# A matmul loop that opens with VectorE's pair of tiles: head, casts and transfers rearranged

## The chip, the cores and the metric

One core of a Trainium2 chip. The metric is the device time of one execution in microseconds (us). The kernel before took 210.7 us (median of 4 runs, 210.26 to 210.95).

## The reference

```python
batch, m, k, n = 16, 512, 1024, 768
def reference(x, weight, sub_value):      # x [16,512,1024], weight [1024,768], sub_value [16,512,768], float32
    return (np.matmul(x, weight) - sub_value).astype(np.float32)
```

The 16 x 512 rows are one flat list of 8,192 rows, so the work is a product of 8,192 x 1,024 by 1,024 x 768, less a matrix of the size of the result.

## The kernel before

The rows form 64 m tiles. With SEGMENTS (L14) and `view` (L128) a segment of j tiles gives each of the 128 partitions j neighbouring rows, so that one transfer of n tiles moves n x 4,096 bytes (x) or n x 3,072 bytes (sub_value, result) in one run per partition. x lands in a ring of 16 tiles (`x_ring`), sub_value in a ring of 32 tiles (`so_ring`); the result of a tile overwrites its sub_value in place and is sent from there. The weight is staged in the last eight slots of `so_ring`.

What happens to one tile `mi`:

1. **Cast.** ScalarE casts x from float32 to float16 (`cast`, L300, L317).
2. **Transpose.** TensorE needs x with k on the partitions. Two ways exist. For most tiles TensorE transposes four blocks of 128 x 128 float32 words (each word two float16 values) against an identity (`transposes`, L322, L335), and ScalarE copies the result from PSUM to SBUF (L348, the "evac"). For the tiles in ON_DVE and their successors, VectorE transposes a pair of two tiles with 16 block transposes (`transposes_dve`, L353, L368), and ScalarE has no evac. There is one buffer for a transposed pair (`xtp_b`, NXTP = 1).
3. **Matmuls.** 16 matmuls of 128 x 384 columns (`matmuls`, L377, L198): four chunks c of k, two halves r of a chunk, two halves of n. They add up in one of three PSUM buffers (`po_b`).
4. **Finish.** VectorE subtracts: PSUM minus `so_ring` into `so_ring` (`finish`, L412, L417).

Each engine has a queue written out by hand (`Queue`, L40); engines meet through semaphores. A wait sits on the instruction that needs it, and all that stands behind it on the same engine waits too. SyncE (SP) issues all transfers in the order of TRANSFERS (L29). `issue` (L241) adds a transfer to SP's queue as soon as the program text has passed what frees its slot, and it carries its waits: an x transfer waits for the casts of the 16 tiles before, a sub_value transfer for the landing of the results that it overwrites (or for the weight's casts, L285), a result for its last finish.

TensorE's work has a head and a loop. The head (L438 to L473) computes tiles 0 to 3 by hand, interleaved so that each weight chunk is used by several tiles as it lands, with 26 idle matmuls on zeros that keep TensorE busy meanwhile. Tiles 4 and 5 are TensorE-transposed but stand in the pair buffer (EARLY = 4), so that the loop body has one shape; a memset on GpSimd (L476) and two tiny casts at the end (L499) fill up counters for that. The loop (LOOP = (4, 6, 10), L517) is ten turns of six tiles, 4 to 63: a pair from `xtp_b` and four tiles of TensorE's own. VectorE transposes the nine pairs 10, 16, ..., 58. Transposes of tile `mi + 2` stand between the matmuls of tile `mi` (L490); a pair's VectorE transposes are spread behind the finishes of tiles 5, 4 and 3 places before it, six, six and four (L502 to L506).

The loop counts its semaphore targets in registers, with one jump back per turn (`emit_loop`, L69, L101).

## Time and profile before

| | us |
|---|---|
| median of 4 runs (lowest, highest) | 210.7 (210.26, 210.95) |
| the profiled execution's own time | 210.76 |
| its span, first to last instruction | 208.9 |
| TensorE matmul busy / VectorE / ScalarE | 195.4 / 128.1 / 108.8 |
| DMA queue of the transfers, share of 16 engines' span | 97.8% (87.03 MB) |
| last matmul ends | 201.4 |
| last transfer issued, landed | 202.4, 5.2 us later |

The profiled execution stands 0.06 us above the median. Busy matmuls overlap in the profile: a matmul of 384 columns is shown with 326 ns, but in a dense stretch one starts every 0.1625 us. The 1.8 us between span and time lie outside the first and last instruction.

### The profile page before, as it was taken

The page shows a single profiled execution, that of the slowest core. Times are in us where ns is not written, and L with a number is a line of the kernel's source. Part 1 is how long each engine was busy: PE and PEld are TensorE (multiplying, and loading weights), DVE is VectorE, ACT ScalarE, POOL GpSimd, SP SyncE. Part 2 cuts the span into 40 slices and gives each one's busy share as a digit, 9 for nine tenths or more (in the row PEclk, how much of TensorE's full clock was granted, in tenths as well). Part 3 has the DMA queues.
Part 4 walks back from the last instruction along what each step waited for, and adds up shares of the span by engine and source line. Part 5 has one row for each costly group of instructions (what it writes and reads, how often), then busy time and mean ns, then how long its engine had stood idle before and what let it go on. Part 6 is the DMA issues. An engine that isn't in the chain of part 4 may idle for free.

```text
span 208.9 us, 2614 instructions
## 1 busy us (share of the span) xinstructions
PE 195.4 (94%) x1234; PEld 75.5 (36%) x700; DVE 128.1 (61%) x224; ACT 108.8 (52%) x113; POOL 1.0 (0%) x7
## 2 busy tenths in 40 slices
PE   6999799969999999999999999999999999999950
PEld 0233243324434434433442443343344344334310
DVE  2323314975993895597499389369749929943330
ACT  4555758507574761853845667173574646516300
POOL 1000000000000000000000000000000000000000
PEclk9999999999999999999999999999999999999997
DMA  6999999999999999999999999999999999999992
GB/s 234 410 427 434 443 417 436 455 427 434 423 464 408 346 445 448 450 414 406 474 425 417 438 409 442 447 450 416 433 445 392 445 438 433 414 447 438 408 419 119
DMA packets 5620, 87.08 MB, mean 417 GB/s; under 512 B 624, under 2 KB 624, under 8 KB 2032
## 3 DMA queue, kind: packets, MB, share of 16 engines
q1 hardware_dynamic: 5616, 87.03, 97.8%
q8 instruction: 1, 0.02, 0.0%
q14 instruction: 3, 0.02, 0.0%
HBM read 61.87 MB, written 25.17 MB: 417 GB/s over the span
## 4 chain that ended last, share of the span: by engine, by line
PE 75%; DMA 13%; DVE 6%; SPq 3%; issue 1%; DVEq 0%
PE po_b L198 67%; DMA so_ring<-in_sub_value_dram 13%; PE pt_b L335 8%; DVE xtp_b L368 3%; DVE so_ring L417 2%; SPq L298 2%; SPq L262 1%; SPq L553 0%; DVEq L59 0%; SPq L138 0%
## 5 line engine op out<-in xcount | busy, mean ns | idle before, releaser
L198 PE MATMUL po_b<-w_sb,xt_b 128*128 128x384 f16 x704 | 126.0, 326 | 0.9 <-DVE w_sb L265 0.5
L417 DVE TENSOR_TENSOR so_ring<-po_b,so_ring 128x768 f32<-128x768 f32 x64 | 60.6, 956 | 59.5 <-PE po_b L198 38.7
L348 ACT COPY xt_b<-pt_b 128x1024 f16<-128x1024 f16 x44 | 44.5, 1012 | 64.2 <-PE pt_b L335 63.3
L368 DVE STREAM_TRANSPOSE xtp_b<-x16p_b 32x256 f32<-32x256 f32 x144 | 62.7, 435 | 2.3
L198 PE MATMUL po_b<-w_sb,xtp_b 128*128 128x384 f16 x320 | 61.3, 326 | 1.9 <-DVE xtp_b L368 1.7
L397 PEld LDWEIGHTS <-xt_b 128*128 128x128 f16 x352 | 34.4, 98 | 58.5 <-issue 55.0
L317 ACT CAST x_b<-x_ring 128x1024 f16<-128x1024 f32 x46 | 47.2, 1048 | 4.7 <-DMA x_ring<-in_x_dram 4.7
L335 PE MATMUL pt_b<-ident,x_b 128*128 128x128 f32 x184 | 47.5, 273 | 1.5 <-ACT x_b L317 1.4
L335 PEld LDWEIGHTS pt_b<-ident,x_b 128*128 128x128 f32 x184 | 25.4, 141 | 44.7 <-issue 36.8
L317 ACT CAST x16p_b<-x_ring 128x1024 f16<-128x1024 f32 x18 | 18.8, 1046 | 16.1 <-DMA x_ring<-in_x_dram 16.1
L397 PEld LDWEIGHTS <-xtp_b 128*128 128x128 f16 x160 | 15.7, 98 | 20.4 <-issue 18.3
L265 DVE CAST w_sb<-so_ring 128x768 f16<-128x768 f32 x8 | 4.1, 557 | 11.3 <-DMA so_ring<-in_weight_dram 11.3
L198 PE MATMUL po_b<-idle_x,idle_w 128*128 128x512 f16 x26 | 8.0, 458 | 1.7 <-POOL idle_x L178 1.7
L348 ACT COPY xtp_b<-pt_b 128x1024 f16<-128x1024 f16 x2 | 2.0, 1012 | 2.5 <-PE pt_b L335 2.5
L317 ACT ACT_TABLE_LOAD x1 | 1.3, 1283 | 0.9 <-SPq L138 0.9
L427 PEld LDWEIGHTS <-idle_w 128*128 128x128 f16 x4 | 0.4, 99 | 1.7 <-POOL idle_x L178 1.7
L187 DVE TENSOR_TENSOR ident<-along,across 32x32 f32<-32x32 f32 x4 | 0.7, 183 | 0.1
L179 DVE MEMSET ones<- 128x32 f32 x1 | 0.1, 85 | 1.0 <-SPq L138 1.0
L178 POOL MEMSET idle_x<- 128x512 f16 x1 | 0.5, 529 | 0.0
L499 ACT CAST stub<-ident 128x1 f16<-128x1 f32 x2 | 0.4, 194 | 0.0
L184 DVE STREAM_TRANSPOSE across<-along 128x32 f32<-128x32 f32 x1 | 0.2, 211 | 0.0
L177 POOL MEMSET idle_w<- 128x128 f16 x1 | 0.2, 204 | 0.5 <-SPq L138 0.5
(7 smaller groups left out, 0.9 us busy)
## 6 DMA issues: line engine op xcount, KB each, us to landing
so_ring<-in_sub_value_dram SPq DMA_DIRECT2D x7, 3072.0 KB, 24.2
x_ring<-in_x_dram SPq DMA_DIRECT2D x5, 4096.0 KB, 23.8
out_dram<-so_ring SPq DMA_DIRECT2D x6, 3072.0 KB, 29.0
x_ring<-in_x_dram SPq DMA_DIRECT2D x2, 2048.0 KB, 27.1
so_ring<-in_weight_dram SPq DMA_DIRECT2D x4, 768.0 KB, 8.1
x_ring<-in_x_dram SPq DMA_DIRECT2D x1, 3072.0 KB, 28.9
out_dram<-so_ring SPq DMA_DIRECT2D x1, 2688.0 KB, 26.6
x_ring<-in_x_dram SPq DMA_DIRECT2D x2, 1024.0 KB, 24.8
```

Source lines behind the costliest of these rows:

```text
L178: pool.add(lambda: nc.gpsimd.memset(idle_x, 0.0), then=count("idle"))
L187: dve.add(lambda here=here: nc.vector.tensor_tensor(out=ident[here, here], in0=along[here], in1=across[here], op=mybir.AluOpType.is_equal, ...
L198: return nc.tensor.add_instruction(mybir.InstMatmult(name=nc.get_next_instruction_name(), engine=full.engine, ins=list(full.ins), outs=lis ...
L262: sp.add(lambda st=st, at=at: nc.sync.dma_start(out=st, in_=w_c[at]), then=(sem, 16))
L265: lambda at=at, r=r, st=st: nc.vector.tensor_copy(out=w_sb[:, at, r], in_=st[:, r]),
L298: sp.add(lambda here=here, there=there: nc.sync.dma_start(out=here, in_=there), waits, (sem, 16))
L317: act.add(lambda: nc.scalar.copy(out=to, in_=x_in), waits, count("cast"))
L335: pe.add(lambda: nc.tensor.transpose(words, from_, ident), waits, count("turn") if last else None)
L348: act.add(lambda: nc.scalar.copy(out=to, in_=pt_b[:, b]), waits, count("evac"))
L368: dve.add(lambda: nc.vector.transpose(xt[b * Q : (b + 1) * Q, :, a * Q : (a + 1) * Q], x16[a * Q : (a + 1) * Q, :, b * Q : (b + 1) * Q],), ...
L397: pe.add(lambda weights=weights: nc.tensor.ldweights(weights, tile_position=(0, 0)), [w for w in waits if w[0] in ready])
L417: dve.add(lambda: nc.vector.tensor_tensor(out=o, in0=po[:, :, :NS], in1=o, op=mybir.AluOpType.subtract), [landed["s", mi], (counter["mul"] ...
```

## The change

- **No head.** The pair (0, 1) goes to VectorE, so the loop begins at tile 0. VectorE transposes eleven pairs (0, 6, ..., 60). EARLY, the memset, the stub casts and the interleaved head go. x of tile 1 is cast by VectorE, so that both casts of pair 0 run at once; they have a counter of their own, `both`.
- **The loop** (`emit_turns`) has turns that start at tiles 0, 6, ..., 60 and is left in the middle of the fourth tile of the eleventh turn, after half of tile 63. Its body is two blocks, so each turn has two jumps. Tile 63's last two chunks stand behind it.
- **TensorE's transposes** stand in whole tiles: those of `mi + 2` behind chunk 2 of the pair's two tiles, those of the next two tiles together in the middle of the fourth tile.
- **Casts** have new places in ScalarE's order (CAST_AHEAD). Six of the eight weight casts go to ScalarE. The loop's pair tile waits for each half chunk of the weight by itself.
- **Transfers:** 34 in place of 39. The weight comes in two, behind x of tiles 0 to 3; sub_value 32 to 39 now stands ahead of x 32 to 39, and x 48 to 55 is split.
- **Idle matmuls:** 35 at the start, none later (26 before).

```diff
-SEGMENTS = [(0, 1), (1, 7)] + [(at, 8) for at in range(8, 64, 8)]
+SEGMENTS = [(0, 2), (2, 6)] + [(at, 8) for at in range(8, 64, 8)]
+IDLE = 34
+CAST_AHEAD = (6, 7, 4, 4, 3, 3)
+W_ON_ACT = {(0, 0), (0, 1), (1, 0), (1, 1), (2, 0), (3, 0)}
+PERIOD, CUT = 6, (3, 2)
-ON_DVE = frozenset(range(10, 60, 6))
+ON_DVE = frozenset(range(0, 64, 6))
 TRANSFERS = [
+    ('x', 0, 2), ('x', 2, 2), ('w', 0, 2), ('w', 2, 2), ('x', 4, 4), ('s', 0, 2), ('s', 2, 6),
+    ('x', 8, 4), ('x', 12, 4), ('s', 8, 8), ('x', 16, 8), ('s', 16, 8), ('x', 24, 8),
+    ('o', 0, 2), ('o', 2, 6), ('s', 24, 8), ('s', 32, 8), ('x', 32, 8), ('x', 40, 8),
+    ('o', 8, 8), ('o', 16, 8), ('s', 40, 8), ('x', 48, 2), ('x', 50, 6), ('o', 24, 8),
+    ('s', 48, 8), ('x', 56, 8), ('s', 56, 8), ('o', 32, 8), ('o', 40, 8), ('o', 48, 8),
+    ('o', 56, 5), ('o', 61, 2), ('o', 63, 1),
...
+    def emit_turns(self, turns, cut):
...
+        nc.regs_mov(turn, 1)
+        nc.br("turn_first", engines=engines)
+        with nc.body("turn_first", valid_engines=engines):
+            self.emit(first[:cut], bound, after)
+            nc.br_cmp(turn, len(turns), on_true="turn_done", on_false="turn_second", comp_op="IS_EQ", engines=engines)
+        with nc.body("turn_second", valid_engines=engines):
+            self.emit(first[cut:], lambda n, sem, v: bound(n + cut, sem, v), lambda n, sem: after(n + cut, sem))
+            nc.regs_alu(turn, turn, 1, op=mybir.AluOpType.add)
+            nc.br("turn_first", engines=engines)
+        nc.switch_bb("turn_done")
...
+    def cast_w(c):
+        sem, value, first = w_landed[c]
+        for r in range(2):
+            name = "w_act" if (c, r) in W_ON_ACT else "w"
+            to, from_ = w_sb[:, c, r], so_ring[:, first + r]
+            if name == "w":
+                dve.add(lambda to=to, from_=from_: nc.vector.tensor_copy(out=to, in_=from_), [(sem, value)], count(name))
+            else:
+                act.add(lambda to=to, from_=from_: nc.scalar.copy(out=to, in_=from_), [(sem, value)], count(name))
...
-        act.add(lambda: nc.scalar.copy(out=to, in_=x_in), waits, count("cast"))
+        name = "both" if first in ON_DVE else "cast"
+        if mi == 1:
+            dve.add(lambda to=to, from_=x_in: nc.vector.tensor_copy(out=to, in_=from_), waits, count(name))
+        else:
+            act.add(lambda: nc.scalar.copy(out=to, in_=x_in), waits, count(name))
...
         for r in range(2):
+            if mi % PERIOD == 0:
+                waits.append(w_at[c, r])
...
+    idle(IDLE)
+    cast(0)
+    cast(1)
+    for f in transposes_dve(0):
+        f()
+    cast(2)
+    cast(3)
+    for c in range(n_c):
+        cast_w(c)
+    casts = {0: [6, 7], 1: [4], 2: [5]}
+    for mi in range(8, n_mt):
+        casts.setdefault(mi - CAST_AHEAD[mi % PERIOD], []).append(mi)
...
+    for mi in range(n_mt):
+        for c in range(n_c):
+            if (mi % PERIOD, c) == CUT:
+                marks.append(len(pe.ops))
+                for t in (mi + 1, mi + 2):
+                    if t < n_mt:
+                        transpose_tile(t)
+            matmuls(mi, c)
+            if c == TURN_AT and mi % PERIOD < 2:
+                transpose_tile(mi + TA)
+        for t in casts.get(mi, []):
+            cast(t)
+        finish(mi)
```

The rest of the main loop (VectorE's transposes behind the finishes of 5, 4 and 3 tiles before a pair) is as before.

## The prediction

> **What bounds the kernel now.** I read the page's chain first, then its slices, then the last microseconds of DMA. The chain names TensorE for three quarters of the span:

> ```profile
> PE 75%; DMA 13%; DVE 6%; SPq 3%; issue 1%; DVEq 0%
> ```

> The slices say that the transfers are never short of work either; only the first and last slice fall below full:

> ```profile
> DMA  6999999999999999999999999999999999999992
> GB/s 234 410 427 434 443 417 436 455 427 434 423 464 408 346 445 448 450 414 406 474 425 417 438 409 442 447 450 416 433 445 392 445 438 433 414 447 438 408 419 119
> ```

> The end decides between the two. This is DMA in 40 slices from 202.4 us, when the last transfer (384 KB of tile 63) is issued, to the end of the span:

> ```profile
> DMA  9999998989899984311121201101000000000000
> GB/s 451 395 395 507 413 413 376 451 376 395 338 395 470 376 338 188 132 75 75 56 94 75 94 38 56 56 38 75 38 19 0 0 0 0 0 0 0 0 0 0
> ...
> out_dram<-so_ring SPq DMA_DIRECT2D x1, 384.0 KB, 5.2
> ```

> The engines stay full for 2.5 us after that issue (202.4 to 204.9), so older transfers were ahead. Then a few engines work alone to 207.3. In the trace's landing times, the last transfer's 16 parts land at 205.1 to 205.6 on thirteen engines and at 206.8, 207.5 and 207.64 on three. **The end is the slowest DMA engine's backlog.** Without a backlog the transfer would land about 2.4 us after its issue: 1.0 to the first packet (x of tile 0: issued 0.94, first packets 1.5 to 2.0), 8 packets of 3,072 B at 0.121 us, 0.35 from the last packet to its landing. That is 204.8. So TensorE could end some 2.8 us later and be hidden, if no engine's queue runs dry.

> TensorE has no slack of its own: each six tiles take 17.35 us at full clock.

> ```profile
> 57.41:74.76 17.35, 17.35 (x115) 6.95 (x64) 12.83 (x23) 9.72 (x10) 0.00 (x0) 1.00 0.99 408
> ```

> That is 96 matmuls of 0.1625 us (2.60 a tile) and 16 transposes of 0.109 (0.44 a tile). What sets its place is an early VectorE chain (VectorE's timeline, 34 to 46 us):

> ```profile
> 33.98 1.82 DVE L417 TENSOR_TENSOR so_ring<-po_b,so_ring 128x768 f32<-128x768 f32 x2 [7.07 <-DMA so_ring<-in_sub_value_dram]
> 35.72 2.67 DVE L368 STREAM_TRANSPOSE xtp_b<-x16p_b 32x256 f32<-32x256 f32 x6
> 38.40 0.96 DVE L417 TENSOR_TENSOR so_ring<-po_b,so_ring 128x768 f32<-128x768 f32 x1
> 39.38 2.68 DVE L368 STREAM_TRANSPOSE xtp_b<-x16p_b 32x256 f32<-32x256 f32 x6
> 42.08 0.96 DVE L417 TENSOR_TENSOR so_ring<-po_b,so_ring 128x768 f32<-128x768 f32 x1
> 43.07 1.80 DVE L368 STREAM_TRANSPOSE xtp_b<-x16p_b 32x256 f32<-32x256 f32 x4
> ```

> VectorE waits 7.07 us for sub_value of tiles 4 to 7, then needs 10.9 us to finish pair 10; TensorE starts it at 45.11, and is dense from there to 201.40.

> **Transfers.** Bytes are equal. Packets per engine go from 312 to 288 and landings from 39 to 34 (the weight keeps two runs per partition and transfer half). A packet costs 8 ns beside its bytes: 3,072 B take 121 ns and 32,768 B take 1,213, so 0.03677 ns a byte and 8 ns left. 24 x 8 + 5 x 9 ns = **-0.24 us** on every engine. No queue runs dry: SP's longest new dependence is sub_value 32 to 39 on the landing of results 0 to 7 at some 81 us, with 3.1 MB (to 88.5) queued behind it; x 24 to 31 waits for the cast of tile 15 (some 50 us) with work to 62.9; sub_value 40 to 47 waits to 122.8 with work to 130; and the last full result, of tile 55, is ready at 181.4 with work to 193.

> **Start.** Landings by bytes, from before's (1.31 MB at 6.09 us, 3.93 at 12.47, 5.77 at 16.83, 8.91 at 24.13, 11.01 at 29.04, 17.83 at 45.99, 42.99 at 105.79): x0-1 5.45, x2-3 8.1, w0-1 11.9, w2-3 15.6, x4-7 20.5, s0-1 22.4, s2-7 27.8, s8-15 46.0. Pair 0: ScalarE's cast 1.05 (VectorE's beside it is 0.56 for 768 columns, 0.75 by width) to 6.55; 16 transposes at 0.45 to 13.8; matmuls from 14.0, as 44.88 to 45.11 gave 0.23 before. ScalarE casts weight halves from 11.9 at 0.8 each (1.05 by width; ends 0.56, VectorE's row, and 1.05), so chunk 1 is ready at 15.1 and chunk 3 at 17.2, and tile 0 ends at 18.2. Tiles 1 to 5 follow with their eight-word transposes; cast 5, behind casts 6, 7, evac 3 and cast 4 on ScalarE (20.5 + 5 x 1.05 = 25.7), costs 0.2. Tile 5 ends at 32.7. Meanwhile VectorE: finish 0 at 22.4, finish 1, six transposes to 27.0, finish 2 at 27.8 with s2-7, six more, finish 3, four: 34.4, so **tile 6 starts at 34.6**, after a stall of 1.9 us, which takes the place of the 1.7 before pair 10.

> The 35 idle matmuls end at 10.9 (eight 0.427 apart up to 5.05, as before, then 27 at 0.216), so TensorE idles for 3.1 us; the trace shows full clock through 1.7 us idle at 43 and nothing longer. At the start half clock lasted 3.4 us (1.67 to 5.05); a second such stretch would lose up to half of that, 1.7 us, in tiles 0 and 1, and the stall of 1.9 ahead of tile 6 covers it (bounds 0 and 1.7, taken 0). [...]

> **Loop.** From 34.6 four tiles and 16 transposes bring tile 10 at 46.7 (before 45.11) and tile 12 at 51.9. VectorE's finish 8 waits for s8-15 to 46.0; 0.96 + 2.7 + 0.96 + 1.8 later, with gaps, pair 12 is done at 52.4: **tile 12 starts at 52.6**. Then 52 tiles x 2.60 + 34 on TensorE's own x 0.44 = 150.1: 202.7. One more wait: x 32 to 39 now lands at 105.8 (98.5 before), and ScalarE's cast of tile 32 then ends at 106.85 where TensorE wants it at 106.6; **+0.25**. Later casts and pairs keep 0.9 us or more (pair: 10.35 from the finish five tiles ahead, against 11.27 that TensorE needs). TensorE ends at **203.0**, 1.6 later than before, although it has 16 transposes (1.75 us) fewer.

> Two jumps a turn: before's jump back takes 0.21 us at 58.80, and the first matmul behind it starts at 62.45 without a gap, so the sequencer is 3.65 us ahead. I take 0; bounds are 0 and, with no lead, 21 x 0.21 = 4.4. [...]

> **Sum.** Tile 63's finish ends at 204.0, its transfer lands at 206.4 at the earliest. The slowest engine's backlog gives 207.64 - 0.24 = 207.4. I take a further 0.1 off: the slowest engine fell back by 1.2 us when a 16 KB instruction packet ran on it at 28.8, in TensorE's first turn, and TensorE's program loses its head; but the next slowest (two 8 KB packets, about 1.0 each, at 50 and 146, where VectorE's program goes on) was only 0.12 less late and stays. 207.3: -0.35. From the profiled 210.76 that is 210.4, and from the median 210.35; **210.4**. What this kernel's measurement can tell is about 0.3%, 0.6 us: below 210.1 is faster, above 211.3 slower.

> **Rivals.**
> - *Late engines vanish* (20%): if the instruction packets fall elsewhere, all engines end with the thirteen, 205.6 - 0.24; then tile 63 itself sets the end, 206.4: -1.2, **209.5**. For it: the lags come from a handful of packets. Against: VectorE's program is longer, not shorter.
> - *TensorE's arrival takes over* (slower, 25%): pair 12's VectorE chain, which starts at a landing, decides the start of tile 12. Each microsecond beyond 53.5 (0.9 later than worked out) is added to the end. With the 1.2 us that one engine lost before added to s8-15, and 1.0 to the wait at tile 32, TensorE ends at 205.2 and the end is 208.6: +0.95, **211.7**; with the jumps' bound on top, 214. For it: three waits in a row with margins under 1 us.
> - *TensorE's transposes are the gain* (5%): if no early VectorE chain held it, 1.75 us fewer would end TensorE at 199.7. It gives no more than the first rival, 209.5, as the backlog stays.
> - *Forecast* (50%): the engines stay the bound, 210.1 to 210.7.

> Faster 0.26 (first and third rival and a little of the forecast's edge), same 0.48, slower 0.26. The range reaches from the first rival, a little beyond, to a little above the second: 209.4 to 212.

> **What would show it.** Right: DMA full from slice 2 to the last, the last transfer landing over 3 us after its issue, a few engines alone at the end, tile 6 at 34 to 35 us and tile 12 near 52.6 behind VectorE, the last matmul near 203. Wrong: a last landing 2.4 us after issue (TensorE bounds), gaps between matmuls at the jumps, PEclk under 9 after 14 us, a DMA slice under 8 in the middle.

## The result and the profile after

The changed kernel takes 211.16 us (median of 39 runs, 210.47 to 211.55), the kernel before 210.85 us (59 runs, 210.26 to 211.35): ratio 1.0015, 95% interval 1.0011 to 1.002. It is slower by 0.31 us where the prediction had it faster by 0.35; that is inside the range given, and under the 0.3% that the prediction set as its bound.

Every run gives two numbers, the time and the span from the first to the last instruction. Means over all runs of the study (before was run beside each experiment; a run's span is on record to 0.1 us, so its difference is good to 0.05):

| | runs | time | span | time less span (lowest to highest) |
|---|---|---|---|---|
| before | 143 | 210.85 | 209.03 | 1.820 (1.77 to 1.88) |
| after | 41 | 211.14 | 209.07 | 2.070 (2.02 to 2.12) |

So 0.25 us of the 0.29 between the means lie **outside the span**, where neither the profile nor the prediction's sum looks, and 0.04 inside. The profiled runs say the same: span 208.93 after, 208.94 before, time 210.99 and 210.76.

The page of after, its chain and its slices:

```profile
DMA  6999999999999999999999999999999999999983
GB/s 212 420 438 418 460 411 442 455 455 397 414 489 402 351 443 445 420 445 425 458 420 422 423 438 428 408 461 425 433 433 441 433 428 423 442 428 438 416 368 161
DMA packets 5156, 87.07 MB, mean 417 GB/s; under 512 B 544, under 2 KB 544, under 8 KB 1568
...
q8 instruction: 1, 0.02, 0.0%
...
PE 72%; DMA 19%; DVE 3%; SPq 2%; issue 1%; DVEq 0%
```

The transfers still fill every slice from the second on, and the first moves less than before (212 against 234 GB/s). The 16 KB instruction packet (q8), which was to go, is still there; it ran at 32.75 us. The chain's DMA share grew from 13 to 19%, because it now goes back through VectorE to s8-15, as the timeline of after (0 to 60 us, VectorE's transposes and the matmuls that wait for them) and its chain (40 to 54 us) show:

```profile
6.82 7.18 DVE L380 STREAM_TRANSPOSE xtp_b<-x16p_b 32x256 f32<-32x256 f32 x16 [0.38 <-ACT x16p_b L335]
14.21 1.46 PE L203 MATMUL po_b<-w_sb,xtp_b 128*128 128x384 f16 x8 [2.99 <-DVE xtp_b L380]
...
32.58 1.79 DVE L380 STREAM_TRANSPOSE xtp_b<-x16p_b 32x256 f32<-32x256 f32 x4
34.58 2.11 PE L203 MATMUL po_b<-w_sb,xtp_b 128*128 128x384 f16 x12 [1.79 <-DVE xtp_b L380]
```

```profile
5.91 40.20 DMA so_ring<-in_sub_value_dram
...
46.16 0.44 issue
46.59 0.96 DVE so_ring L426
...
52.62 0.45 DVE xtp_b L380
53.08 0.19 issue
53.26 0.81 PE po_b L203 x4
```

In brackets is the idle time before the instruction and what ended it: TensorE idles 2.99 us ahead of pair 0 and 1.79 ahead of pair 6. Pair 12 follows 7.1 us after the landing of s8-15 at 46.11, with 0.44 us of "issue" ahead of VectorE's subtraction that nothing in the profile explains. From 53.26 TensorE is dense. One turn of six tiles:

```profile
58.85:76.19 17.34, 17.34 (x113) 6.53 (x64) 12.62 (x22) 9.62 (x10) 0.00 (x0) 1.00 0.99 408
```

(columns: span, then busy us and count of PE, PEld, DVE, ACT and POOL, granted clock, DMA share, GB/s) is full at clock 1.00, as before. DMA from the last issue (204.49 us) to the span's end, in 40 slices of 0.11 us:

```profile
DMA  1212121699999989310011110000000000000000
GB/s 56 111 55 111 55 111 55 249 443 443 443 387 415 415 332 387 111 55 28 28 55 55 55 55 28 0 0 0 0 0 0 0 0 0 0 0 0 0 0 0
...
out_dram<-so_ring SPq DMA_DIRECT2D x1, 384.0 KB, 3.2
```

(Such a view counts a packet, its time and its bytes, in the slice in which it starts.) Here most engines wait for tile 63: from 204.8 to 205.3 three of the sixteen work, then its packets come at once. Fourteen engines are done by 206.78 and two end alone, at 207.52 and 207.65 (before: 207.51 and 207.64). So the end is still the slowest engine's, 3.2 us after the issue, but the cover in front of it has shrunk from 2.8 us to 0.9.

### The profile page after: what moved, and what is told of

It reads as the page before. It is cut to its first block, busy times and chain, and to the rows that moved or that the text cites. A ratio compares the mean times of both kernels' runs of the same rounds, so it can differ in the third digit from the quotient of the medians.

```text
span 208.9 us, 2636 instructions
## 1 busy us (share of the span) xinstructions
PE 194.9 (93%) x1227; PEld 69.5 (33%) x681; DVE 139.8 (67%) x251; ACT 107.5 (51%) x112; POOL 0.9 (0%) x6
## 4 chain that ended last, share of the span: by engine, by line
PE 72%; DMA 19%; DVE 3%; SPq 2%; issue 1%; DVEq 0%
PE po_b L203 65%; DMA so_ring<-in_sub_value_dram 19%; PE pt_b L353 7%; DVE xtp_b L380 2%; SPq L300 2%; DVE so_ring L426 1%; SPq L268 1%; SPq L527 0%; DVEq L57 0%; SPq L145 0%
## 5 line engine op out<-in xcount | busy, mean ns | idle before, releaser
L203 PE MATMUL po_b<-w_sb,xt_b 128*128 128x384 f16 x672 | 112.6, 326 | 0.0
L380 DVE STREAM_TRANSPOSE xtp_b<-x16p_b 32x256 f32<-32x256 f32 x176 | 76.6, 435 | 3.0 <-ACT x16p_b L335 0.4
L360 ACT COPY xt_b<-pt_b 128x1024 f16<-128x1024 f16 x42 | 41.5, 1013 | 69.2 <-PE pt_b L353 68.1
L335 ACT CAST x_b<-x_ring 128x1024 f16<-128x1024 f32 x42 | 41.9, 1050 | 12.8 <-DMA x_ring<-in_x_dram 12.8
L406 PEld LDWEIGHTS <-xtp_b 128*128 128x128 f16 x176 | 17.2, 98 | 50.2 <-issue 34.2
L335 ACT CAST x16p_b<-x_ring 128x1024 f16<-128x1024 f32 x21 | 21.0, 1047 | 5.9 <-DMA x_ring<-in_x_dram 5.9
L353 PE MATMUL pt_b<-ident,x_b 128*128 128x128 f32 x168 | 23.6, 273 | 0.0
L353 PEld LDWEIGHTS pt_b<-ident,x_b 128*128 128x128 f32 x168 | 20.4, 141 | 8.0 <-issue 7.3
L203 PE MATMUL po_b<-idle_x,idle_w 128*128 128x512 f16 x35 | 9.6, 442 | 1.7 <-POOL idle_x L183 1.7
L310 ACT CAST w_sb<-so_ring 128x768 f16<-128x768 f32 x6 | 4.6, 828 | 2.5 <-DMA so_ring<-in_weight_dram 2.5
L308 DVE CAST w_sb<-so_ring 128x768 f16<-128x768 f32 x2 | 1.0, 558 | 1.7 <-DMA so_ring<-in_weight_dram 1.7
## 6 DMA issues: line engine op xcount, KB each, us to landing
x_ring<-in_x_dram SPq DMA_DIRECT2D x3, 2048.0 KB, 27.8
```

The lines of the kernel that those rows point to most:

```text
L203: return nc.tensor.add_instruction(mybir.InstMatmult(name=nc.get_next_instruction_name(), engine=full.engine, ins=list(full.ins), outs=lis ...
L308: dve.add(lambda to=to, from_=from_: nc.vector.tensor_copy(out=to, in_=from_), [(sem, value)], count(name))
L310: act.add(lambda to=to, from_=from_: nc.scalar.copy(out=to, in_=from_), [(sem, value)], count(name))
L335: act.add(lambda: nc.scalar.copy(out=to, in_=x_in), waits, count(name))
L353: pe.add(lambda: nc.tensor.transpose(words, from_, ident), waits, count("turn") if last else None)
L360: act.add(lambda: nc.scalar.copy(out=xt_b[:, d], in_=pt_b[:, b]), waits, count("evac"))
```

## The experiments

Each time is a median; comparisons are with runs of before on the same chip. Spans and "time less span" are means of all runs of a kernel (standard error of a span mostly 0.05 to 0.09, after 0.03, before 0.02). Three questions were put: does TensorE now set the end (theory T), does the start lose what the packets save (theory S), and what is longer outside the span (theories L, the layout of the code, W, SyncE's waits and program, and D, VectorE's program). A line of three dots stands for lines of an edit that are left out.

### Does TensorE set the end?

**e5_after_late**: VectorE fills 4 x 128x352 ahead of the last subtraction.

```
+    spare = sbuf("spare", [P, 4, 352], F32)
...
+        if mi == n_mt - 1:
+            for k in range(4):
+                dve.add(lambda k=k: nc.vector.memset(spare[:, k], 0.0), [(counter["mul"], mul_at[mi])])
```

> The changed kernel with four memsets of 128x352 on VectorE ahead of the last finish, which delay only the last tile's result, by 1.5 to 2 us. In the profiled execution the last transfer could have landed at 206.7 where the slowest DMA engine set 207.65, a margin of 0.9. Theory S (the DMA engines' backlog is the usual bound, TensorE has this margin): +0.6 to +1.1 us against the changed kernel. Theory T (TensorE's arrival is already the bound in most executions): the whole delay, +1.5 us or more.

Measured: 211.75 us (5 runs), span 209.68. The timeline of its end:

```profile
203.62 1.47 DVE L429 MEMSET spare<- 128x352 f32 x4 [1.75 <-PE po_b L204]
205.01 0.90 DVE L430 TENSOR_TENSOR so_ring<-po_b,so_ring 128x768 f32<-128x768 f32 x1
```

The last issue moved by 1.44 us, to 205.93, the span by 0.61, and all 16 engines landed at 208.04 to 208.24, so that 0.83 us were covered. Theory T had the whole delay at the end.

**e6_before_late**: the same lines in before.

> The kernel before with the same four memsets ahead of the last finish. Its last transfer, issued at 202.4, could land near 204.6 and lands at 207.64 behind the slowest engine's backlog: a margin of 3 us. If that reading is right, the delay costs nothing, ratio 0.9995 to 1.0005; if the last tile's arrival sets the end, +1.5 us or more, ratio 1.007.

Measured: 210.81 us (12 runs), span 209.03, time less span 1.82. Last issue 203.72 in place of 202.41, last landing 207.62: before covers all of it, as the prediction had it.

**e7_tensor_early**: s8-9 as a transfer of its own, so that pair 12 starts sooner, and x32 ahead of s32.

```
-    ... ('s', 8, 8), ...  ('s', 32, 8), ('x', 32, 8),
+    ... ('s', 8, 2), ('s', 10, 6), ...  ('x', 32, 8), ('s', 32, 8),
```

> The changed kernel with sub_value 8 to 15 in two transfers (two tiles, then six) and x 32 to 39 ahead of sub_value 32 to 39 again (35 transfers). VectorE's finish of tile 8 no longer waits for eight tiles to land, so TensorE should start tile 12 some 1.2 us earlier and end 1.3 to 1.7 us earlier, near 202; the transfers cost 0.07 us more. Theory T: the time falls by 0.2 to 0.4 us, ratio to the kernel before 0.9995 to 1.0005. Theory S: it stays or rises by 0.07 us, ratio 1.0015 to 1.002.

Measured: 211.22 us (12 runs), ratio 1.0018 (1.001 to 1.0027), span 209.12. DMA from its last issue, 203.32 us, on:

```profile
DMA  9486596989978322121010100001000000000000
...
out_dram<-so_ring SPq DMA_DIRECT2D x1, 384.0 KB, 4.4
```

TensorE ends 1.17 us earlier (202.30), there is backlog again ahead of the last transfer, and the end stays at 207.76. **Theory T falls.**

**e2_after_half** and **e3_before_half**: the same edit in after and in before.

```
-        for r in range(2):
+        for r in range(1):
...
-                    stop=(c == n_c - 1 and r == 1),
+                    stop=(c == n_c - 1),
...
```

> The changed kernel with half of its matmuls left out (the second half r of each chunk), so the result is not the reference's and TensorE is never the bound; the transfers are the same. Theory S: the DMA engines' backlog alone sets the end, so the time stays within 0.2 us of the changed kernel's, ratio to the kernel before 1.000 to 1.0015. Theory T: without TensorE's late arrival the saved packets show, ratio 0.9985 to 0.9995.

> The kernel before with half of its matmuls left out in the same way (the result is not the reference's). All theories in which the DMA engines' backlog bounds the kernel before: ratio 0.999 to 1.0005. If TensorE had a part in its end: 0.998 or less. The difference between this and the run of the changed kernel's half is what the two transfer lists cost by themselves: theory S +0.1 us or more for the changed one, theory T -0.2 us.

Measured: 211.0 us (span 208.92) and 210.8 us (span 208.96), 11 runs each. TensorE ends at 194.6 and 196.7, the last landings stay at 207.62 and 207.82. With TensorE out of the way, the two sets of transfers differ by 0.05 us, with a standard error of 0.10: not by 0.35. That lies between what T (0.2 less) and S (0.1 or more) expected.

### Does the start lose it?

**e1_split_start**: x0 and x1 as two transfers. **e8_early_and_split**: the same in e7.

```
-    ('x', 0, 2), ('x', 2, 2), ...
+    ('x', 0, 1), ('x', 1, 1), ('x', 2, 2), ...
```

> The changed kernel with its first transfer (x of tiles 0 and 1, packets of 8,192 bytes) split into two of one tile each (4,096 bytes). Theory S (the start): in the changed kernel's trace the first packet of each DMA engine takes about 0.95 us, before 0.45, so that all engines begin full work some 0.35 us later, which eats the 0.24 us saved on packets. Then this kernel's landings stand 0.25 to 0.35 us ahead of the changed kernel's (x 12 to 15 near 38.5 instead of 38.85) and its time is 0.2 to 0.3 us below it, ratio to the kernel before 0.9995 to 1.0005. Theory T (the tail): TensorE's arrival, 2.1 us later than before, sets the end in many executions; then the time stays at the changed kernel's, ratio 1.001 to 1.002.

> As e7, and the first transfer of x split into two of one tile each (36 transfers). Theory S alone: as the run with the split start, ratio 1.000. Theory T alone: as e7. Both together: below either, 0.998 to 0.9995.

Measured: 210.97 us (11 runs), ratio 1.0001 (0.9992 to 1.001), span 208.83; and 210.89 us (12), ratio 1.0006 (0.9996 to 1.0015), span 208.96. The times are those that S forecast, but not in the way that S had it: in e1's trace 0.80 MB have moved by 5 us (after 0.94, before 1.08; a packet under way counts by its share), and x12-15 lands at 39.74 (after 38.85, S 38.5). So the start itself is slower, although the span is shorter. Time less span varies from run to run, from 1.77 to 2.21 in e1, as it does in neither before nor after.

**e4_after_half_16k**: on e2, x0-3, s0-3 and s4-7 (and the results) as transfers of four tiles, 33 in all.

```
-SEGMENTS = [(0, 2), (2, 6)] + ...
+SEGMENTS = [(0, 4), (4, 4)] + ...
-    ('x', 0, 2), ('x', 2, 2), ('w', 0, 2), ('w', 2, 2), ('x', 4, 4), ('s', 0, 2), ('s', 2, 6),
+    ('x', 0, 4), ('w', 0, 2), ('w', 2, 2), ('x', 4, 4), ('s', 0, 4), ('s', 4, 4),
...
```

> The changed kernel with half of its matmuls left out (the result is not the reference's) and its first transfers made of four tiles (x 0 to 3 in one transfer, packets of 16,384 bytes; sub_value and results 0 to 3 and 4 to 7 likewise, 33 transfers). Theory S: the first packet of each engine doubles again, to 1.7 to 2.0 us, and the end moves by +0.5 to +0.9 us against the run of the changed kernel's half. Theory T and a theory in which the first packet costs a fixed time: 0 to -0.1 us.

Measured: 210.62 us (11 runs), ratio 0.9986 (0.9977 to 0.9995), span 208.68, time less span 1.92; 0.80 MB by 5 us. The largest first packets, and the shortest span: **theory S falls.**

**h2_mixed** (run last, on g1 below): x0-1, w0-1, x2-3, w2-3 in turn, casts to match.

```
-    ('x', 0, 2), ('x', 2, 2), ('w', 0, 2), ('w', 2, 2), ...
+    ('x', 0, 2), ('w', 0, 2), ('x', 2, 2), ('w', 2, 2), ...
...
```

> Edit, on after with the shared result counter: the start transfers x0-1, w0-1, x2-3, w2-3, so that x and weight alternate as in before, with the casts of weight parts 0 and 1 ahead of those of tiles 2 and 3; same packets. Theory X (two x transfers in a row, with their 8,192 byte packets, cost the 0.3 us that after is behind at 5 us, 0.94 MB to 1.08 MB): bytes moved by 5 us rise to about 1.05 MB, the span falls by about 0.25 to 208.85, time 210.7. If what is lost at the start is made up near 70 us, where all kernels pause, or the start is not the cause: span 209.1, time 210.95.

Measured: 210.98 us (11 runs), span 209.12. The order is not it. Packets that start from 0 to 5 us, in slices of 0.125 us, before and then h2:

```profile
DMA  0000000000000009995579998979999599993929
...
DMA packets 245, 1.14 MB, mean 229 GB/s; under 512 B 16, under 2 KB 16, under 8 KB 245
```

```profile
DMA  0000000000000009900008419499693994939969
...
DMA packets 124, 1.02 MB, mean 203 GB/s; under 512 B 0, under 2 KB 0, under 8 KB 0
```

The zeros behind h2's first packets are not idle engines: no packet starts there, because the first ones, of 8,192 bytes, take up to 1.33 us. By the packets' own times eight engines are at work from 2.0 us and all sixteen from 2.9; in after all sixteen are from 2.3, with first packets of 0.34 to 1.24 us. Before's, of 4,096 bytes, take 0.16 to 0.69. By 5 us the nine traces with x0-1 in front have moved 0.92 to 0.99 MB, h2 0.93, and the seven of before and its variants 1.05 to 1.11: the lag stays, whatever follows x0-1. It does not set the end, as e2 against e3 and e4 show.

### What is longer outside the span?

Counted in the compiled programs, SyncE has 73 instructions in before and 76 in after, VectorE 247 and 273, TensorE 345 and 244. e2 and e3 (TensorE 166 and 225) and e5 and e6 (VectorE 277 and 251) left the difference within 0.06 us of what it was.

**f1_layout**: the loop's second half stands before what follows the loop.

```
-            nc.br_cmp(turn, len(turns), on_true="turn_done", on_false="turn_second", comp_op="IS_EQ", ...)
+            nc.br_cmp(turn, len(turns), on_true="turn_second", on_false="turn_done", comp_op="IS_LT", ...)
```

> Edit: in after, the loop's two halves lie next to each other in the program (the compare at the end of the first half names the second half first), so that the code behind the loop no longer lies ahead of the second half's 76 instructions; nothing that an engine executes is changed, and no transfer. In the runs so far, after's time less its span is 2.07 us and before's 1.82, while the spans differ by 0.06 only. Theory L (the part outside the span is longer because TensorE, at the end, jumps over the second half to the program's end, which must be fetched): time less span falls to 1.82, the time to about 210.9 (ratio to before 1.000). Theory W (SyncE's end, three more result counters waited for) and theory D (VectorE's program, 26 instructions longer): time less span stays at 2.07, time 211.15, ratio 1.0015.

Measured: 211.16 us (12 runs), time less span 2.018. L explains 0.05 at most, and neither after's trace nor f1's has a packet from 208.5 to 212 us, so that no fetch is shown there.

**f2_before_waits**: three waits more at SyncE's end.

```
+    for name in ("turn", "mul", "evac"):
+        nc.sync.wait_ge(counter[name], 1)
```

> Edit: in before, three more waits of SyncE at the end, on counters that have long been reached, so that SyncE's block there has six instructions as in after, not four. Theory W: time less span rises from 1.82 to about 2.0, time to about 211.05, ratio 1.001. Theories L and D: time less span stays at 1.82, time 210.85, ratio 1.000.

Measured: 211.0 us (12 runs), ratio 1.0009 (0.9998 to 1.002), time less span 1.929 (1.82 to 2.01). W gains.

**f3_before_dve26**: 26 fills at VectorE's end.

```
+    pad = sbuf("pad", [P, 26], F32)
+    for n in range(26):
+        dve.add(lambda n=n: nc.vector.memset(pad[:, n : n + 1], 1.0))
```

> Edit: in before, 26 fills of one column of 128x1 on VectorE behind its last subtraction, into a tile of their own: VectorE's program then has 273 instructions as in after, not 247. They end some 1.6 us after VectorE's last subtraction and before the last landing, so that the span should stay. Theory D: time less span rises from 1.82 to 2.07, time to about 211.1, ratio 1.0012. Theories L and W: time less span stays at 1.82, time 210.85, ratio 1.000.

Measured: 210.84 us (11 runs), time less span 1.818. **D falls.**

**f4_after_33**: one transfer less.

```
-    ... ('x', 48, 2), ('x', 50, 6), ...
+    ... ('x', 48, 8), ...
```

> Edit: in after, the transfers of x48-49 and x50-55 are one transfer of eight tiles: 33 transfers instead of 34, and SyncE's program has 74 instructions instead of 76. It is issued when the tile that the later one waited for has been read, so that x48 lands some us later; TensorE reaches m tile 48 near 158 us, and x48 can then be late. Theory W: time less span falls from 2.07 to about 1.9; theories L and D: it stays at 2.07. By bytes and packets alone the span falls by under 0.01 us (no packet changes its size, one completion less); if x48 comes late, by at most some 2 us, TensorE's own margin of 0.9 us decides whether the span grows.

Measured: 211.53 us (5 runs), span 209.70, time less span 1.826. Outside it loses the whole 0.25; inside, x48 lands at 147.0 and TensorE waits for its tile:

```profile
150.15 1.46 PE L203 MATMUL po_b<-w_sb,xt_b 128*128 128x384 f16 x8 [1.25 <-ACT xt_b L360]
```

The last transfer is issued 1.6 us later than in after (206.10) and the span 0.63 longer: 0.98 us of cover, against e5's 0.83.

**g1_after_shared**: the six last result transfers count on one semaphore; 34 transfers as in after, SyncE 73.

```
+        late = tag[0] == "o" and tag[1] >= NSO
         for one in lanes:
-            if one["tags"] <= known:
+            if one.get("late") if late else one["tags"] <= known:
...
```

> Edit: in after, the six result transfers from o32 on (whose slots nothing overwrites) count on one semaphore, so that SyncE waits at the end for five others instead of ten; the 34 transfers and their order stay, SyncE's program has 73 instructions instead of 76. So far time less span by the instructions of SyncE's program: 73 (before) 1.82 us, 74 (the 33 transfers) 1.83, 75 (before with three waits) 1.93, 76 (after) 2.07. Theory W (this part grows with SyncE's program or with its waits at the end): 1.82 us, with the span of after (209.07) a time of 210.9, ratio to before 1.000. If the eleven counters or the transfers themselves made it: 2.07, time 211.15.

Measured: 210.96 us (12 runs), ratio 1.0007 (0.9999 to 1.0016), time less span 1.833, span 209.16. **W holds**: the transfers are those of after, and the 0.25 us are gone.

**g2_before_mid**: f2's three waits ahead of s48. **g4_before_shared**: g1's edit in before.

> Edit: in before, the same three waits on long reached counters as in the kernel with waits at the end, but ahead of the transfer of s48, where SyncE has time: SyncE's program has 75 instructions, its block at the end four as in before. If the length of SyncE's whole program counts: time less span 1.93 us as with the waits at the end, time 210.95. If only the waits at the end count: 1.82, time 210.85.

> Edit: in before, the result transfers from o32 on count on one semaphore: SyncE waits at the end for fewer counters, its program has 71 instructions instead of 73. If time less span grows only above some length: 1.82 us as before, ratio 1.000. If each wait or instruction costs its part: 1.7 or less, ratio 0.9994.

Measured: g2 210.9 us (12 runs), time less span 1.953; g4 210.91 us (12 runs), 1.813. With the same 75 instructions, waits in the middle (g2, 1.953) and at the end (f2, 1.929) gave nearly the same; what time less span followed was the length of SyncE's program, and only above 74 instructions. All kernels in one table:

| SyncE instructions | time less span |
|---|---|
| 71 | g4 1.81 |
| 73 | before 1.82, e3 1.81, e6 1.82, f3 1.82, g1 1.83, h1 1.82, h2 1.83 |
| 74 | f4 1.83, g3 1.82 |
| 75 | e4 1.92, f2 1.93, g2 1.95 |
| 76 | after 2.07, e2 2.01, e5 2.05, f1 2.02 |
| 77 | e1 2.07, e7 2.04, spread over 1.77 to 2.21 |
| 78 | e8 1.97, spread over 1.78 to 2.14 |

One trace row may bear on the cause. DMA of e1 from 208.5 to 212 us, behind the span's end at 209.1:

```profile
DMA packets 1, 0.01 MB, mean 2 GB/s; under 512 B 0, under 2 KB 0, under 8 KB 0
...
q14 instruction: 1, 0.01, 0.9%
```

An instruction packet of 8,192 bytes runs there, at 211.0 (e1) and 210.9 (e7), in the traces of the two kernels with 77 instructions and in no other. The profiled runs of these two had 2.18 and 2.04 us outside the span; that of e8, with 78, had 1.82, near the least of its spread. That such a packet lengthens the part outside is the author's guess and not shown, as the kernels with 75 and 76 have none.

### What does a packet cost at the end?

**h1_quarters** (on g1): packets of two tiles instead of eight (of two instead of four in x8-15) for tiles 8 to 47.

```
+        if 8 <= first < 48:
+            rows = flat[at * P : (at + n) * P]
+            return rows.rearrange("(s p j) c -> p s j c", p=P, j=2)
...
```

> Edit, on after with the shared result counter: the transfers of m tiles 8 to 47 have packets of two m tiles in place of eight (x8-11 and x12-15: in place of four), 8,192 and 6,144 bytes in place of 32,768 and 24,576. Same transfers, same bytes, 352 packets more on each engine. Theory P (the backlog's end moves by what the packets cost, 8 to 9 ns each, as the prediction's sum had it): the span grows by 2.8 to 3.1 us, time about 213.9. Theory N (a packet's own time is not what bounds the backlog, since the memory or what else the engines share does): the span stays within 0.5 us of 209.1, time 211.0 to 211.4.

Measured: 211.58 us (7 runs), span 209.76. Its page:

```profile
DMA packets 10788, 87.07 MB, mean 416 GB/s; under 512 B 544, under 2 KB 544, under 8 KB 6688
...
q1 hardware_dynamic: 10784, 87.03, 98.4%
```

There are 352 packets more on each engine. By the packets' usual durations (the median of each size) that is 2.77 us, and the span grew by 0.66 (against 209.10, the mean of 88 runs of after, f1, g1, e7 and h2): **1.9 ns a packet at the end, not 8 to 9**. That is near theory N, though above its 0.5 us. Part of the rest was slack: the time by which packets ran over their usual duration is 0.80 us per engine here, 1.20 to 1.60 in the traces of those five kernels, and in o56-60 the first landing came 1.4 us later than in h2 (203.47 to 202.03), the last only 0.5 (205.34 to 204.88).

### Both together

**g3_split_shared**: g1 with e1's split start.

> Edit: after with x0 and x1 as transfers of their own and with the shared result counter: 35 transfers, 74 instructions on SyncE. Theory W: time less span 1.83 us and without the spread from run to run that the split start showed (1.77 to 2.21); with the span of the split start (208.83, interval of some 0.17) the time is about 210.7, ratio 0.999, so faster than both kernels. If the split start's spread has another cause: 2.07 and 210.9.

Measured: 210.94 us (12 runs), ratio 1.0001 (0.999 to 1.0012), time less span 1.818 (1.78 to 1.86), span 209.07. The spread is gone; the kernel is as fast as before, not faster. Over e1, e8 and g3 together the split start's span is 208.95 (35 runs, standard error 0.05), 0.15 below that of the 88 runs; g3 alone, at 209.07, shows no gain.

## Why the prediction was wrong, step by step

**Right: what bounds.** The backlog of the slowest engine ends the span in both kernels (207.64 and 207.65), and TensorE's later end is hidden (e2, e6, e7). Before's cover was worked out as 2.8 us; e6 spends 1.3 of it for nothing. After's cover is 0.83 to 0.98 (e5, f4). Two readings of this part are slightly off: before's first packets start at 1.96 to 2.20 us, not at 1.5 to 2.0, and the terms for a transfer without a backlog add up to 2.32 us, not 2.4 (e5's last one landed 2.11 to 2.31 after its issue).

**Right, nearly to the digit: the start and the loop.**

| step | predicted | measured |
|---|---|---|
| x0-1, w0-1, w2-3, x4-7 land | 5.45, 11.9, 15.6, 20.5 | 5.72, 11.94, 15.68, 20.54 |
| s2-7, s8-15, x32-39 land | 27.8, 46.0, 105.8 | 27.82, 46.11, 105.60 |
| TensorE starts pair 0, pair 6 | 14.0, 34.6 | 14.21, 34.58 |
| tile 12 starts | 52.6 | 53.26 |
| TensorE ends | 203.0 | 203.47 |

Tile 12 is late by 0.66 us: 0.44 of "issue" before VectorE's subtraction, 0.11 of s8-15's landing, the rest gaps; the rival that named this chain put its point at 53.5. The wait for x32 (+0.25) did not come, as TensorE reached tile 32's transposes at 107.25, 0.6 after the cast. No matmul of after shows a gap at a jump (from 53.26 us on TensorE has no gap at all), so 0 was right for them; a turn takes 17.34 us against 17.35.

The second stretch at half clock, taken as 0, was a real risk: it came in some runs, and cost no time. Eleven traces of after and its variants have all the matmuls. In seven, with 2.14 to 2.99 us idle before pair 0 (after 2.99), the clock stayed full; in four, with 3.22 to 3.95, it was half for 3.4 or 6.8 us from about 15 us on. So the idle time, 3.1 us in the prediction, varied by 1.81 us from trace to trace, and 3.22 us of it was followed by the half clock. The stretch from 16 to 18 us of after and of g1 (3.22 us idle, granted clock third from the end):

```profile
16.00:18.00 2.00, 1.42 (x11) 0.76 (x7) 0.73 (x2) 1.40 (x3) 0.00 (x0) 1.00 0.95 410
```

```profile
16.00:18.00 2.00, 1.22 (x5) 0.37 (x2) 0.97 (x2) 1.51 (x2) 0.00 (x0) 0.50 1.07 459
```

In g1 the half clock lasted 6.8 us, twice what the prediction allowed for. Tile 6 started 0.91 us later than in after (35.49), tile 12 only 0.23 (53.49): the stalls ahead of both took it up. The four traces with the half clock have a granted clock of 0.978 to 0.985 over the whole run; of after's 41 runs the 16 with at most 0.986 took 211.14 us in the mean, the other 25 took 211.15.

**Wrong: "24 x 8 + 5 x 9 ns = -0.24 us on every engine".** The sum of the packets' usual durations did fall by 0.245 us per engine. But a packet's own duration is not what the end moves by: at h1's 1.9 ns, 24 packets are 0.05 us, and e2 against e3 gives 0.05, with a standard error of 0.10. The slope was read from durations of single packets, where the end of a backlog on 16 engines was meant. What takes up the difference is shown only in part (h1).

**Wrong: "I take a further 0.1 off".** The 16 KB instruction packet stayed. It is absent in the trace of e2, whose TensorE program has 166 instructions, and there in e3 with 225 and after with 244. The three of 8 KB stayed too, at 50.38, 84.91 and 141.25 us (before 50.30, 87.15 and 145.66); that it is VectorE's program that they carry was the author's reading, and no run shows it.

**Wrong, and most of the result: "From the profiled 210.76 that is 210.4".** This carries the 1.8 us around the span over unchanged. They became 2.07, by SyncE's 76 instructions (g1, f2, g2, f4). No rival had it.

So the sum that the runs give is +0.25 outside the span, -0.05 for packets, 0 for the instruction packet, and some +0.1 inside that is left over, where the measured span is 0.04 longer. The split start, 0.15 shorter over three kernels, may point to x0-1 as one transfer; but g3 alone does not gain, and it moves fewer bytes by 5 us, not more, so this is not shown. It also stays open what SyncE's 75th instruction sets off.

## What to carry to other kernels

Where two kernels differ by tenths, take time less span from every run first: a profile cannot explain what lies outside it. Count each engine's instructions, SyncE's waits too, and where SyncE's program is long, let results whose landing nobody else waits for count on one semaphore (76 to 73 instructions gained 0.25 us, 73 to 71 nothing). And price a packet by an experiment that adds hundreds of them, since the duration of one was not what the end of this full backlog moved by (1.9 ns a packet in h1, where the durations gave 7.9).
